# Attention outputs summed by accumulating transfers; weight casts, differences and value products moved

## The chip, the cores and the metric

The kernel runs on one core of a Trainium2 chip. A core has five engines that run side by side, each through its own queue in order: TensorE (matrix products, transposes), VectorE (elementwise work, scans), ScalarE (activations and copies), GpSimd or POOL (small elementwise work, and transfers that its software describes) and SyncE or SP (which only issues transfers). Transfers can be issued from SP's, ScalarE's and POOL's queue; the instruction that issues one waits in its queue until its data are there. Instructions wait for one another by semaphores. The metric is device time in microseconds (us) of one execution.

## The reference

The reference is one layer of a model with 1024 tokens of width 1024, in float32. Two branches run on the same normalised input, a gate merges them, and a feed-forward block follows:

```
u = rmsnorm(x) @ w_in          # q,k,v (8 heads of 64); f,i,q,g (4 heads of 128); 2 gates of 1024
o_sb = stick_breaking_attention(q_sb, k_sb, v_sb)
o_hg = rmsnorm(hgrn2(silu(q_hg), f_raw, i_hg)) * silu(g_hg)
merged = sigmoid(gate_sb + b) * (o_sb @ w_o_sb) + sigmoid(gate_hg + b) * (o_hg @ w_o_hg)
h = x + merged @ w_out
out = rmsnorm(h + square(relu(rmsnorm(h) @ w_ff1)) @ w_ff2)
```

The attention has no softmax. With z = q.k / 8, the weight of key s for query t is sigmoid(z_ts) times the product of (1 - sigmoid(z_tj)) over the keys j between s and t, for s < t only. The output of a head is the weights times v.

## The kernel before

Precision. Each float32 operand of a large product is kept as two halves: hi, a cast on ScalarE (hi_copy, line 156), and lo, the difference between the value and its hi on VectorE (lo_sub, line 161). A product is then three matmuls (hi.hi, hi.lo, lo.hi; the helper three). All matmuls are recorded at line 128 and all transposes at line 131, so the profile tells them apart by tile names.

Order. The program is traced by Python; each instruction gets a place on its engine from a planner that goes by program order and estimated times. after(a, b) forces a behind b on the same engine, without a wait. Two lanes order TensorE: the main lane (scores, transposes, value products of the attention) and the fill lane, a Stream of jobs that project the normalised input by slices of w_in. st.advance(n, upto) runs n steps of the Stream; a projection job has nine steps, eight of them with six matmuls of 512 columns. When a job starts, the Stream loads and splits the weights of the next one (prefetch). Raw weights lie in two buffers, tag "raw", their halves in two buffers each, tags "whi" and "wlo". All loads are issued from SP's queue, in the order in which they are traced (load, line 136).

Stages. First the input is normalised, transposed (norm_transpose, tiles xnt, xnh, xnl) and projected to v (pjv, units wv), with head 0's q and k. Then the attention runs over 64 items (head, block of 128 queries), the blocks in the order 7, 0, 6, 1, 5, 2, 4, 3. For an item, scores makes z, and ScalarE its two sigmoids bt and rm (lines 786 and 789); weights runs the running product as a scan on VectorE (line 808) and multiplies (line 169); turn transposes the weights (tiles pw) and splits them into wTh and wTl; values, called when both query blocks of a 256-query column qc are turned, multiplies them with v (tile po). The jobs in this stage are q and k of the heads 1 to 7 (units wqk), the f and q projections of the recurrence (wf, wq), and two of ten "raw" gate units (wga8 and wga9). The HGRN2 recurrence with the job of i (unit wi, four pieces) follows, then gates, the output projection, and the feed-forward.

The value products. v is stored as hi and lo side by side in the 128 columns of the stationary operand, so po is 128 x 256: partitions 0 to 63 hold the part with v's hi and 64 to 127 that with its lo. Their sum is the output. values copies the one half on ScalarE to the partitions of the other (line 886, tile ot), adds on VectorE (line 887, tile osb, one slot for two heads), and after the eighth column block of a pair of heads a transfer on POOL's queue stores osb to the buffer od (line 896), which is loaded again in the gate stage.

The raw gate units. A RawUnit has two raw pieces, ra and rb. split makes hi and lo of ra. split_t makes a difference rb = ra - rb (1024 wide, recorded at line 1243), a second one of its halves (512 wide, line 1243), and hi and lo of that (tile t). In the Stream it is owed from the start of the job before and paid when that job reaches step 6, all at once, the first difference behind the latest turn's lo (or, in the recurrence, behind its latest product).

The pieces of wi. hg_levels(0), the first head of the recurrence, calls u_i.split(1), which loads and splits the first piece; its cast has no place behind anything on ScalarE.

Of the kernel before, what the change touches and what calls it, by code (L numbers as in the profile page):

```python
# [10 lines left out]
F32R = mybir.dt.float32r  # L11
# [3 lines left out]
ALU = mybir.AluOpType  # L15
# [4 lines left out]
P = 128  # L20
T = 1024
D = 1024
NT = T // P
# [4 lines left out]
DHS = 64  # L28
# [11 lines left out]
def kernel(  # L40
# [19 lines left out]
    nc = tc.nc  # L60
# [14 lines left out]
    def slot(name, dt=F32):  # L75
        return spool.tile([P, 1024], dt, tag="s", name=name)

    def slot_n(name, n, dt=F32):

        if n <= 512:  # L80
            return hpool.tile([P, 512], dt, tag="h", name=name)
        return slot(name, dt)

    def bank(name):
        return psum.tile([P, 512], F32, tag="p", name=name)
# [7 lines left out]
    def dram(name, shape):  # L93
        return scratch.tile(shape, F32, tag=name, name=name)

    class Lane:
        def __init__(self):
            self.ends = []
            self.last = None
            self.gates = ()  # L100
# [4 lines left out]
    def after(ins, earlier):  # L105
        if earlier is not None and earlier.ins is not ins.ins:
            tc.add_manual_dep(ins.ins, earlier.ins.name, NOSYNC, reason="issue order")
        return ins

    def open_block(name):  # L110
        cur[0] = name
        lane = lanes[name]
        lane.gates = (lane.last,)
        if name == "main":
            lane.ends.append(lane.last)
        else:
            ends = lanes["main"].ends
            lane.gates += tuple(ends[-AHEAD : len(ends) - AHEAD + 1])
# [8 lines left out]
    def matmul(*a, **k):  # L127
        return pe(nc.tensor.matmul(*a, **k))  # L128
# [24 lines left out]
    hi_behind, hi_last, turn_hi = [None], [None], [None]  # L153

    def hi_copy(dst, src):
        hi_last[0] = after(in_turn("act", nc.scalar.copy(dst, src)), hi_behind[0])  # L156

    def lo_sub(dst, src, hi):
        return in_turn(
            "dve",  # L160
            nc.vector.tensor_tensor(out=dst, in0=src, in1=hi.bitcast(F32), op=ALU.subtract),  # L161
        )

    def hi_lo(h, l, src):
        hi_copy(h, src)
        return lo_sub(l, src, h)

    def mul(out, a, b):
        return nc.vector.tensor_tensor(out=out, in0=a, in1=b, op=ALU.mult)  # L169
# [140 lines left out]
    def norm_transpose(acts, half, b0, n, between=None):  # L310

        banks = {}

        def turn_block(kt, b):
            if kt not in banks:
                banks[kt] = bank(f"xnt{half}{kt}_{b0}")[:, 0 : n * P]
            open_block("main")
            transpose(
                banks[kt][:, b * P : (b + 1) * P],
                xt[4 * half + b0 + b][:, kt * P : (kt + 1) * P],  # L320
            )

        ahead = 6 if between else 0
        for kt in range(ahead):
            turn_block(kt, 0)
        if between:
            between()
        for kt in range(KT):
            hi, lo = acts.t.get((half, kt // 2)) or acts.make(half, kt // 2)
            cs = slice(kt % 2 * 512 + b0 * P, kt % 2 * 512 + (b0 + n) * P)  # L330
            for b in range(n):
                if b > 0 or kt >= ahead:
                    turn_block(kt, b)
            pb = banks[kt]
            g = prm[:, G1 + kt : G1 + kt + 1]
            in_turn("act", nc.scalar.activation(hi[:, cs], pb, AF.Identity, scale=g))
            in_turn(
                "dve",
                nc.vector.scalar_tensor_tensor(
                    out=lo[:, cs],  # L340
                    in0=pb,
                    scalar=g,
                    in1=hi[:, cs].bitcast(F32),
                    op0=ALU.mult,
                    op1=ALU.subtract,
                ),
            )
# [85 lines left out]
    class Unit:  # L433
# [5 lines left out]
        def split_t(self):  # L439
            pass  # L440
# [46 lines left out]
    class Stream:  # L487
# [36 lines left out]
        def step(self):  # L524

            if self.gen is None:
                if self.pos >= len(self.jobs):
                    return False
                self.steps = 0
                self._start()  # L530
            self.steps += 1
            if self.owed_t and self.steps == 6:
                self.owed_t.split_t(hg_level[0] or turn_lo[0])
                self.owed_t = None
            open_block("fill")
            if next(self.gen, StopIteration) is StopIteration:
                self.gen = None
                self.pos += 1
            return True
# [11 lines left out]
    st = Stream()  # L551
# [88 lines left out]
    def norm1(tbs):  # L640
        for tb in tbs:
            t = xt[tb]
            r = token_rstd(t, f"n1_{tb}", slot(f"n1scr{tb}"))
            in_turn(
                "dve",
                nc.vector.tensor_scalar(out=t, in0=t, scalar1=r, scalar2=None, op0=ALU.mult),
            )


    vt, qk, osb = {}, {}, {}  # L650
# [9 lines left out]
    def v_stat(h, tb):  # L660
        c = ((tb % 2) * 4 + h % 4) * P
        return vt[h // 4, tb // 2][:, c : c + P]
# [102 lines left out]
    lastsel, turn_lo = [None], [None]  # L765
# [99 lines left out]
    to_come, od = {}, {}  # L865

    def values(h, qc):
        open_block("main")
        tiles = wTt.pop((h, qc))
        nkb = 2 * qc + 2  # L870
        po = bank(f"po{h}_{qc}")[:, 0:256]
        for kb in range(nkb):
            for i in range(2):
                matmul(
                    po,
                    v_stat(h, kb),
                    tiles[kb // 4][i][:, kb % 4, :],
                    start=kb == 0 and i == 0,
                    stop=kb == nkb - 1 and i == 1,
                )  # L880
        pair, r = h // 2, (h % 2) * DHS
        if pair not in osb:
            osb[pair] = slot(f"osb{pair}")
        other = DHS - r
        tmp = slot_n(f"ot{h}_{qc}", 256)[:, 0:256]
        nc.scalar.copy(tmp[r : r + DHS, :], po[other : other + DHS, :])
        nc.vector.tensor_tensor(
            out=osb[pair][r : r + DHS, qc * 256 : (qc + 1) * 256],
            in0=po[r : r + DHS, :],
            in1=tmp[r : r + DHS, :],  # L890
            op=ALU.add,
        )
        to_come[h] = to_come.get(h, NT // 2) - 1
        if r and to_come[h] == 0:
            od[pair] = dram(f"od{pair}", [P, 1024])
            nc.gpsimd.dma_start(od[pair], osb.pop(pair))


    hg, ohg = {}, {}
    hg_sum, hg_level = [None], [None]  # L900
# [115 lines left out]
    def hg_levels(h):  # L1016
# [59 lines left out]
        for _, cs in halves():  # L1076
            after(mul(q[:, cs], q[:, cs], dec[:, cs]), pairs[3])
        if h == 0:
            u_i.split(1)
        yield  # L1080
        for l in range(7):
            H = 1 << l
# [159 lines left out]
    def sub(out, a, b):  # L1242
        return nc.vector.tensor_tensor(out=out, in0=a, in1=b, op=ALU.subtract)
# [40 lines left out]
    class RawUnit(Unit):  # L1284


        late = True

        def __init__(self, cb):
            dmas = [  # L1290
# [15 lines left out]
            hi_lo(h, l, ra)  # L1306
            self.hl = [(h, l)]

        def split_t(self, behind=None):
            if len(self.hl) == 1:  # L1310
                ra, rb = self.raw
                after(sub(rb, ra, rb), behind)
                sub(rb[:, 512:], rb[:, 512:], rb[:, 0:512])
                t = slot(f"{self.name}t", F32R)
                self.hl.append((t[:, 0:512], t[:, 512:]))
                hi_lo(*self.hl[1], self.raw[1][:, 512:])

    raw_units = [RawUnit(cb) for cb in range(NG)]

# [957 lines left out]
    st.advance(4, 1)  # L2277
    u_v.split(2)
    norm1((2, 3))
    st.advance(3, 1)  # L2280
    norm_transpose(xn, 0, 2, 2)
    u_v.split()
    st.advance(5, 1)
    norm1(range(4, NT))
    st.advance(8, 1)
    norm_transpose(xn, 1, 0, 4)
# [16 lines left out]
    for i, it in enumerate(items):  # L2303
# [16 lines left out]
        r = turn(*it, between)  # L2320
# [7 lines left out]
    st.advance(1, j_q[2])  # L2328
    while ready:
        values(*ready.popleft())  # L2330


    FILL = (3.4, 2.0, 2.6, 2.6, 2.9)
    owed = 0.0
    for h in range(NHG + 1):
        lev = hg_levels(h) if h < NHG else iter(())
        tail = hg_tail(h - 1) if h > 0 else iter(())
        upto = (j_i, j_raw[1], j_raw[6], j_sb[1], j_sb[2])[h]
        going, turned = True, False
        while going:  # L2340
            going = False
            for g in (lev, tail):
                if g is tail and h == 1 and turned and going and st.pos < j_i:
                    continue
                turned = turned or g is tail
                if next(g, StopIteration) is not StopIteration:
                    going = True
                    owed += FILL[h]
                    st.advance(int(owed), upto)
                    owed -= int(owed)  # L2350
        if h + 1 < NHG:
            st.finish(max(j_f[h + 1], j_q[h + 1]))
# [102 lines left out]
```

## Time and profile before

| what | value |
|---|---|
| median of 3 runs | 1439.45 us (1439.32 to 1440.04) |
| profiled execution, its own time | 1439.79 us |
| span of that execution, first to last instruction | 1437.8 us |
| granted TensorE clock | 0.999 |
| TensorE busy | 1424.4 us, 99% |
| VectorE busy | 1118.8 us, 78% |
| ScalarE busy | 678.3 us, 47% |
| POOL busy | 148.0 us, 10% |

PE is TensorE, PEld its loading of weights, DVE VectorE, ACT ScalarE; a q behind a name is the engine's queue, which issues transfers. In a row of the stretches the columns are the window and its length, busy time and count for PE, PEld, DVE, ACT and POOL, the granted clock, the share of the DMA engines and GB/s. In a row of waits: who waited for whom, the total in us, how often, the longest. In a row of the timeline: start, duration, engine, line, operation, result and operands, shapes, count, and in brackets the idle time before it and what ended it. In a row of transfers: size of one, and the median us from issue to landing.

### The profile page before, as it was taken

To read this page: it belongs to the slowest core of one execution; us is meant where nothing else is said; L and a number is where in the kernel's file an instruction comes from. 1 tells how busy PE (TensorE), PEld (TensorE's weight loads), DVE (VectorE), ACT (ScalarE), POOL (GpSimd) and SP (SyncE) were. 2 spreads that over 40 slices of the span, in tenths; PEclk is the share of its full clock that TensorE was granted. 3 is DMA by queue.
4 is the path that set the end of the run, shared out by engine and by line. 5 is a ranking of instruction groups with operands and counts; after the bars stand their busy time and mean duration, and the time that the engine had idled before them with its cause. 6 is when DMAs were issued, how large, how long until landed. Compare 5 with 4: busy or idle time off the path is not lost.

```text
span 1437.8 us, 19221 instructions
## 1 busy us (share of the span) xinstructions
PE 1424.4 (99%) x7056; PEld 1194.5 (83%) x7056; DVE 1118.8 (78%) x1537; ACT 678.3 (47%) x1177; POOL 148.0 (10%) x338
## 2 busy tenths in 40 slices
PE   9999999999999999999999999999999999999998
PEld 8888888888888888888888888888888888888886
DVE  6579999989678898798787898666666758668765
ACT  6356676663233345333244674444444433524343
POOL 3011223210011031000000300000000000000042
PEclk9999999999999999999999999999999999999999
DMA  7124435534015775545477405344446974776835
GB/s 238 27 62 115 110 85 92 89 60 133 22 45 154 232 184 196 167 158 180 153 275 249 176 31 197 131 143 145 161 153 212 349 264 164 259 275 253 274 103 182
DMA packets 161334, 233.54 MB, mean 162 GB/s; under 512 B 26028, under 2 KB 93144, under 8 KB 161240
## 3 DMA queue, kind: packets, MB, share of 16 engines
q1 hardware_dynamic: 145400, 190.11, 39.4%
q0 software_dynamic: 11520, 34.61, 9.4%
q10 hardware_dynamic: 4320, 7.60, 1.4%
q8 instruction: 55, 0.90, 0.3%
q14 instruction: 39, 0.32, 0.1%
HBM read 167.27 MB, written 65.01 MB: 162 GB/s over the span
## 4 chain that ended last, share of the span: by engine, by line
PE 92%; DVE 4%; ACT 1%; DMA 1%; issue 1%; POOL 0%; SPq 0%; DVEq 0%; ACTq 0%; POOLq 0%
PE pm L128 21%; PE pX L128 9%; PE pW L128 6%; PE pY L128 6%; PE pjqk L128 5%; PE gX L128 4%; PE gY L128 4%; PE pga L128 3%; PE pys L128 3%; PE pji L128 3%; PE pyh L128 3%; PE pjq L128 3%; PE pjv L128 3%; PE sl L128 3%; PE pwX L128 2%; PE po L128 2%
## 5 line engine op out<-in xcount | busy, mean ns | idle before, releaser
L156 ACT CAST whid<-w 128x1024 fp32r<-128x1024 f32 x30 | 31.6, 1054 | 154.6 <-PE pm L128 90.0
L808 DVE TENSOR_TENSOR_SCAN rm<-rm,bits 128x511 f32<-128x511 f32 (+7 forms) x72 | 87.1, 1218 | 9.6 <-ACT rm L786 9.4
L128 PE MATMUL pm<-wlod,sh 128*128 128x512 f32 x240 | 93.5, 390 | 0.0
L128 PE MATMUL pm<-whid,sl 128*128 128x512 f32 x240 | 93.4, 389 | 0.0
L128 PE MATMUL pm<-whid,sh 128*128 128x512 f32 x240 | 93.4, 389 | 0.0
L128 PE MATMUL pm<-tl,sh 128*128 128x512 f32 (+1 forms) x210 | 81.3, 387 | 0.0
L128 PE MATMUL pm<-th,sl 128*128 128x512 f32 (+1 forms) x210 | 81.3, 387 | 0.0
L128 PE MATMUL pm<-th,sh 128*128 128x512 f32 (+1 forms) x210 | 81.3, 387 | 0.0
L161 DVE TENSOR_TENSOR wlod<-w,whid 128x1024 fp32r<-128x1024 f32 x30 | 36.7, 1222 | 55.0 <-ACT whid L156 55.0
L161 DVE TENSOR_TENSOR sl<-sa,sh 128x1024 fp32r<-128x1024 f32 x56 | 68.2, 1218 | 0.0
L156 ACT CAST wTh<-pw 128x512 fp32r<-128x512 f32 (+2 forms) x96 | 43.9, 487 | 40.8 <-PE pw L131 39.6
L2091 POOL TENSOR_SCALAR fss<-fss 128x1 f32<-128x1 f32 x8 | 4.5, 560 | 562.1 <-ACT fsc L2086 561.6
L156 ACT CAST sh<-sa 128x1024 fp32r<-128x1024 f32 x56 | 57.2, 1046 | 6.1 <-DMA sa<-ad 6.1
L161 DVE TENSOR_TENSOR wTl<-pw,wTh 128x512 fp32r<-128x512 f32 (+2 forms) x96 | 50.5, 547 | 4.9 <-ACT wTh L156 4.6
L128 PEld LDWEIGHTS pm<-wlod,sh 128*128 128x128 f32 x240 | 45.1, 188 | 10.0 <-DVE wlod L161 0.4
L128 PEld LDWEIGHTS pm<-whid,sh 128*128 128x128 f32 x240 | 45.0, 187 | 9.4
L128 PEld LDWEIGHTS pm<-whid,sl 128*128 128x128 f32 x240 | 45.1, 188 | 9.1
L169 DVE TENSOR_TENSOR bt<-bt,rm 128x511 f32<-128x511 f32 (+7 forms) x72 | 49.0, 684 | 4.2 <-DVE rm L808 0.5
L128 PE MATMUL pX<-sql,t1h 128*128 128x512 f32 x128 | 50.0, 391 | 0.1
L128 PE MATMUL pX<-sqh,t1h 128*128 128x512 f32 x128 | 49.8, 389 | 0.0
L128 PE MATMUL pX<-sqh,t1l 128*128 128x512 f32 x128 | 49.8, 389 | 0.0
L786 ACT ACTIVATE rm<-z 128x511 f32<-128x511 f32 (+4 forms) x96 | 48.0, 500 | 3.5 <-DVE wTl L161 1.0
(933 smaller groups left out, 4475.5 us busy)
## 6 DMA issues: line engine op xcount, KB each, us to landing
w<-in_w_ff_dram SPq DMA_DIRECT2D x72, 512.0 KB, 6.2
sa<-ad SPq DMA_DIRECT2D x56, 512.0 KB, 7.0
ad<-a SPq DMA_DIRECT2D x32, 256.0 KB, 2.1
ad<-s SPq DMA_DIRECT2D x16, 512.0 KB, 5.5
tw<-in_w_out_dram POOLq DMA_DIRECT2D x24, 256.0 KB, 4.0
pr<-pd SPq DMA_DIRECT2D x10, 512.0 KB, 5.1
x<-in_x_dram SPq DMA_DIRECT2D x8, 512.0 KB, 9.9
xnl<-xnh POOLq DMA_DIRECT2D x8, 512.0 KB, 8.9
```

What stands on the lines that cost most here:

```text
L128: return pe(nc.tensor.matmul(*a, **k))
L156: hi_last[0] = after(in_turn("act", nc.scalar.copy(dst, src)), hi_behind[0])
L161: nc.vector.tensor_tensor(out=dst, in0=src, in1=hi.bitcast(F32), op=ALU.subtract),
L169: return nc.vector.tensor_tensor(out=out, in0=a, in1=b, op=ALU.mult)
L786: nc.scalar.activation(rm[:, s0 + c0 - 1 : s0 + m - 1], z[:, c0:m], AF.Sigmoid, scale=-0.125)
L808: sc = nc.vector.tensor_tensor_scan(out=rr, data0=rr, data1=bits[:, 1024 - nk + a : 1024 - nk + b][:, ::-1], initial=rm[:, b : b + 1] if i ...
L2091: nc.gpsimd.tensor_scalar(out=ssq, in0=ssq, scalar1=1.0 / D, scalar2=EPS, op0=ALU.mult, op1=ALU.add)
```

## The change

Four things are changed; no matmul is added or taken out.

- The two halves of the attention output. values now copies the whole of po (128 x 256) on ScalarE into a slot osb of its own for each head. When a head's four column blocks are there, a transfer on POOL's queue adds partitions 64 to 127 onto partitions 0 to 63 within SBUF. The store to od follows per head: keep_attended issues it from ScalarE's queue, right behind the next head's first copy, and for the last head from SP's queue. The adds on VectorE and the tiles ot are gone.
- split_t is paid in three pieces, at steps 4, 6 and 8 of the job before: the first difference, the second, and the cast with its lo; each is put behind the latest turn's lo (or the recurrence's product).
- The cast of u_i's first piece is put behind the last turn's hi cast.
- At the start, the Stream takes four steps instead of three before the second transposes, and four instead of five after them: four matmuls of v's lo move ahead of these transposes.

```diff
--- before.py
+++ after.py
@@ -529,9 +529,10 @@
                 self.steps = 0
                 self._start()
             self.steps += 1
-            if self.owed_t and self.steps == 6:
-                self.owed_t.split_t(hg_level[0] or turn_lo[0])
-                self.owed_t = None
+            if self.owed_t and self.steps in (4, 6, 8):
+                self.owed_t.split_t(hg_level[0] or turn_lo[0], self.steps // 2 - 1)
+                if self.steps == 8:
+                    self.owed_t = None
             open_block("fill")
             if next(self.gen, StopIteration) is StopIteration:
                 self.gen = None
@@ -878,22 +879,25 @@
                     start=kb == 0 and i == 0,
                     stop=kb == nkb - 1 and i == 1,
                 )
-        pair, r = h // 2, (h % 2) * DHS
-        if pair not in osb:
-            osb[pair] = slot(f"osb{pair}")
-        other = DHS - r
-        tmp = slot_n(f"ot{h}_{qc}", 256)[:, 0:256]
-        nc.scalar.copy(tmp[r : r + DHS, :], po[other : other + DHS, :])
-        nc.vector.tensor_tensor(
-            out=osb[pair][r : r + DHS, qc * 256 : (qc + 1) * 256],
-            in0=po[r : r + DHS, :],
-            in1=tmp[r : r + DHS, :],
-            op=ALU.add,
-        )
-        to_come[h] = to_come.get(h, NT // 2) - 1
-        if r and to_come[h] == 0:
-            od[pair] = dram(f"od{pair}", [P, 1024])
-            nc.gpsimd.dma_start(od[pair], osb.pop(pair))
+        if to_come.get(h) is None:
+            to_come[h] = NT // 2
+            osb[h] = slot(f"osb{h}")
+        nc.scalar.copy(osb[h][:, qc * 256 : (qc + 1) * 256], po)
+        to_come[h] -= 1
+        keep_attended()
+        if to_come[h] == 0:
+            nc.gpsimd.dma_start(osb[h][0:DHS, :], osb[h][DHS:P, :], accum_op=ALU.add)
+            summed.append(h)
+
+    summed = []
+
+    def keep_attended(queue=nc.scalar):
+        while summed:
+            h = summed.pop()
+            pair, r = h // 2, (h % 2) * DHS
+            if r == 0:
+                od[pair] = dram(f"od{pair}", [P, 1024])
+            queue.dma_start(od[pair][r : r + DHS, :], osb.pop(h)[0:DHS, :])
 
 
     hg, ohg = {}, {}
@@ -1076,7 +1080,9 @@
         for _, cs in halves():
             after(mul(q[:, cs], q[:, cs], dec[:, cs]), pairs[3])
         if h == 0:
+            hi_behind[0] = turn_hi[0]
             u_i.split(1)
+            hi_behind[0] = None
         yield
         for l in range(7):
             H = 1 << l
@@ -1285,6 +1291,7 @@
 
 
         late = True
+        turned = 0
 
         def __init__(self, cb):
             dmas = [
@@ -1306,14 +1313,18 @@
             hi_lo(h, l, ra)
             self.hl = [(h, l)]
 
-        def split_t(self, behind=None):
-            if len(self.hl) == 1:
-                ra, rb = self.raw
-                after(sub(rb, ra, rb), behind)
-                sub(rb[:, 512:], rb[:, 512:], rb[:, 0:512])
-                t = slot(f"{self.name}t", F32R)
-                self.hl.append((t[:, 0:512], t[:, 512:]))
-                hi_lo(*self.hl[1], self.raw[1][:, 512:])
+        def split_t(self, behind=None, upto=3):
+            ra, rb = self.raw
+            while self.turned < upto:
+                self.turned += 1
+                if self.turned == 1:
+                    after(sub(rb, ra, rb), behind)
+                elif self.turned == 2:
+                    after(sub(rb[:, 512:], rb[:, 512:], rb[:, 0:512]), behind)
+                else:
+                    t = slot(f"{self.name}t", F32R)
+                    self.hl.append((t[:, 0:512], t[:, 512:]))
+                    after(hi_lo(*self.hl[1], rb[:, 512:]), behind)
 
     raw_units = [RawUnit(cb) for cb in range(NG)]
 
@@ -2277,10 +2288,10 @@
     st.advance(4, 1)
     u_v.split(2)
     norm1((2, 3))
-    st.advance(3, 1)
+    st.advance(4, 1)
     norm_transpose(xn, 0, 2, 2)
     u_v.split()
-    st.advance(5, 1)
+    st.advance(4, 1)
     norm1(range(4, NT))
     st.advance(8, 1)
     norm_transpose(xn, 1, 0, 4)
@@ -2328,6 +2339,7 @@
     st.advance(1, j_q[2])
     while ready:
         values(*ready.popleft())
+    keep_attended(nc.sync)
 
 
     FILL = (3.4, 2.0, 2.6, 2.6, 2.9)
```

## The prediction

> **What bounds the kernel now.** I read the page first, then the busy times by stretch, then who waited for whom on TensorE, and last the order of time around each wait that these named.
>
> ```profile
> span 1437.8 us, 19221 instructions
> ...
> PE 1424.4 (99%) x7056; PEld 1194.5 (83%) x7056; DVE 1118.8 (78%) x1537; ACT 678.3 (47%) x1177; POOL 148.0 (10%) x338
> ...
> PE 92%; DVE 4%; ACT 1%; DMA 1%; issue 1%; POOL 0%; SPq 0%; DVEq 0%; ACTq 0%; POOLq 0%
> ```
> ```profile
> 80.00:340.00 260.00, 256.59 (x1454) 220.45 (x1453) 239.41 (x345) 174.53 (x385) 55.84 (x191) 1.00 0.42 96
> ...
> 640.00:660.00 20.00, 20.00 (x90) 16.57 (x89) 17.23 (x27) 8.46 (x11) 1.08 (x2) 1.00 0.51 174
> ```
> ```profile
> PE po L128 <- DVE wTl L161: 2.0, 6, 0.5
> PE po L128 <- ACT wTh L156: 1.4, 2, 0.9
> PE pjqk L128 <- DVE xnl L339: 0.3, 1, 0.3
> PE xnt L131 <- DVE xnl L339: 0.2, 1, 0.2
> PE xnt L131 <- DVE x L646: 0.2, 1, 0.2
> ```
>
> TensorE is the bound: busy 99% of the span and 92% of the chain that ended last. The change takes no matmul out and adds none, so it can win only time in which TensorE stands. That time is small and it sits in the part that the change touches. In the attention stretch (80 to 340 us) TensorE is busy 256.59 of 260.00, so 3.41 us idle, which is just what the first two wait rows sum to (2.0 + 1.4). In the late stretch quoted beside it there is none; there 90 matmuls of 512 columns start in 20.00 us, a pitch of 0.222 us, and the granted clock is 1.00 in both. So a matmul of 256 columns has a pitch of about 0.11 us (half; an estimate). VectorE is busy 239.41 of 260.00 (92%) in that stretch and ScalarE 174.53 (67%): VectorE is the engine that has no room there.
>
> All waits of TensorE in the stretch are of one kind: a value product (po) that wants the hi cast (wTh, ScalarE) or the lo difference (wTl, VectorE) of the weights just transposed. Two places hold most of it. The first:
>
> ```profile
> 102.88 1.21 DVE L1243 TENSOR_TENSOR wga8r<-wga8r,wga8r 128x1024 f32<-128x1024 f32 x1
> ...
> 105.14 0.66 DVE L1243 TENSOR_TENSOR wga8r<-wga8r 128x512 f32<-128x512 f32 x1
> ...
> 106.49 0.69 DVE L161 TENSOR_TENSOR wga8t<-wga8r,wga8t 128x512 fp32r<-128x512 f32 x1
> ...
> 105.83 0.62 ACT L156 CAST wga8t<-wga8r 128x512 fp32r<-128x512 f32 x1 [3.02 <-DVE wga8r L1243]
> ...
> 105.92 0.60 PE L131 MATMUL pw<-ident,bt 128*128 128x128 f32 x4
> 106.99 0.38 PE L128 MATMUL po<-wTh,V 128*128 128x256 f32 x1 [0.48 <-ACT wTh L156]
> 107.83 0.39 PE L128 MATMUL po<-wTl,V 128*128 128x256 f32 x1 [0.46 <-DVE wTl L161]
> ```
>
> Here split_t of gate unit 8 stands in the way. ScalarE waits 3.02 us for the second difference of wga8r, with the casts of the attention weights queued behind that wait; then VectorE runs wga8t's lo before the wTl that TensorE wants. The second:
>
> ```profile
> 320.43 1.05 ACT L156 CAST wih<-wir 128x1024 fp32r<-128x1024 f32 x1 [4.84 <-DMA wir<-in_w_in_dram]
> ...
> 321.89 0.56 DVE L161 TENSOR_TENSOR wTl<-pw,wTh 128x384 fp32r<-128x384 f32 x1 [2.96 <-ACT wTh L156]
> ...
> 321.88 0.60 PE L131 MATMUL pw<-ident,bt 128*128 128x128 f32 x4
> 323.37 0.38 PE L128 MATMUL po<-wTh,V 128*128 128x256 f32 x1 [0.89 <-ACT wTh L156]
> 324.10 0.39 PE L128 MATMUL po<-wTl,V 128*128 128x256 f32 x1 [0.34 <-DVE wTl L161]
> ```
>
> Here ScalarE waits 4.84 us for a load of u_i's first piece, which nobody needs yet, while three casts of the last turns stand behind it; VectorE then waits 2.96 us, and TensorE pays.
>
> The rows of the start, which the moved value products touch:
>
> ```profile
> 16.76 1.07 PE L128 MATMUL pjv<-wvl,xnh 128*128 128x512 f32 x4
> 17.67 0.27 PE L131 MATMUL xnt<-ident,x 128*128 128x128 f32 x1
> 18.14 1.20 PE L131 MATMUL xnt<-ident,x 128*128 128x128 f32 x9 [0.20 <-DVE x L646]
> 19.55 0.83 PE L131 MATMUL xnt<-ident,x 128*128 128x128 f32 x4 [0.21 <-DVE xnl L339]
> ```
>
> Nine transposes take 1.20 us with the last one's 0.27 in it, so their pitch is (1.20 - 0.27) / 8 = 0.116 us.
>
> **The change part by part.**
>
> split_t in three pieces (steps 4, 6 and 8 of the job before, each behind the latest turn's lo). No instruction is added; the 1024-wide difference goes some steps earlier, the cast and its lo some steps later. At the first place the differences are then over when ScalarE comes to the cast, and wga8t's lo is no longer just ahead of wTl. From the first transpose at 105.92 to the second po at 107.83 are 1.91 us; undisturbed it would be 4 x 0.116 + 0.11 = 0.57. That is 1.34 us lost; the idle figures alone give 0.48 + 0.46 = 0.94. I take 1.34, since start to start is what moves everything behind it. What is late next: the raw buffers of units 8 and 9 come free only when the last lo has read them, and SP issues loads in order:
>
> ```profile
> 107.21 1.02 SPq L136 DMA_DIRECT2D wqk4r<-in_w_in_dram  x2
> ...
> 314.67 17.25 SPq L136 DMA_DIRECT2D wir<-in_w_in_dram  x4
> ```
>
> Both start just as a wga lo ends (106.49 + 0.69 = 107.18 for the first). Two steps later in the job is some 3 us later here, for wqk4 and for the first piece of wi. wqk4 is a unit ahead, and wi is wanted by no matmul before the attention is over, so I cost this at nothing; if that cover is gone, it is one wait like those above, about 1.3 us.
>
> u_i's first cast behind the last turn's hi. Nothing added, one order. ScalarE no longer stands at 315.6 to 320.4, the casts of the last turns go when their transposes end, and the po at 323.37 finds its operands. From 321.88 to 324.10 are 2.22 us against 0.57, so 1.65 lost; by idle figures 0.89 + 0.34 = 1.23. I take 1.65. Later the same cast costs its 1.05 us on ScalarE behind the turns, where no po is queued behind it.
>
> The attention outputs.
>
> ```profile
> L886 ACT COPY ot<-po x32: 364/368/371, 93.9 to 332.5; 64x256 f32<-64x256 f32 x32
> L887 DVE TENSOR_TENSOR osb<-po,ot x32: 406/422/429, 94.8 to 332.9; 64x256 f32<-64x256 f32 x32
> ```
>
> ScalarE keeps 32 copies, now 128 partitions instead of 64 at the same 256 columns, which I cost the same, 0.368 us each. VectorE loses 32 adds of 0.422 = 13.5 us out of its 239.41: 92% busy becomes 87%. The po bank also comes free after the copy and not after the add, and a half slot for ot goes while a full slot for osb stays a little longer at each change of head. What it is worth on TensorE: besides the two places above, po waits for wTl four more times, 2.0 - 0.46 - 0.34 = 1.2 us in all. That bounds the gain at 1.2; the bound from the other side is nothing, or a loss where another order puts a 1.2 us lo of a weight ahead of a wTl. These four stand behind casts and differences of the next weights more than behind adds, so I take a quarter, 0.3.
>
> What it adds: 8 accumulating transfers on POOL's queue instead of 4 stores, and 8 stores, 7 on ScalarE's queue and the last on SP's.
>
> ```profile
> xnl<-xnh POOLq DMA_DIRECT2D x8, 512.0 KB, 8.9
> ...
> tw<-tw POOLq DMA_DIRECT2D x8, 256.0 KB, 5.5
> ...
> od<-osb POOLq DMA_DIRECT2D x4, 512.0 KB, 3.5
> ```
> ```profile
> L1379 POOL DMA_DIRECT2D xnl<-xnh x8: 853/878/2217, 431.0 to 529.2; - x8
> ...
> DMA to landing us min/median/max: 4.6/8.9/13.5
> ```
> ```profile
> 324.00 0.33 ACTq L1346 DMA_DIRECT2D pd<-p  x1
> ...
> 299.61 0.37 ACT L886 COPY ot<-po 64x256 f32<-64x256 f32 x1
> ...
> 309.40 0.37 ACT L886 COPY ot<-po 64x256 f32<-64x256 f32 x1 [1.53 <-PE po L128]
> ```
>
> POOL: 8 x 0.878 instead of 4 stores, some 5 us more on an engine that is busy 55.84 of 260.00, and it waits for a ScalarE copy instead of a VectorE add: nothing. ScalarE's sequencer: 7 x 0.33 = 2.3 us of issuing; with 67% busy I take nothing, and 2.3 as the far end, if each stood right ahead of a wTh that TensorE wants. The new wait is the one to watch: the store sits on ScalarE's queue behind the first copy of the next head, and casts and sigmoids of the next items queue behind it. The tightest of the changes of head is quoted: from the copy's end at 299.98 to the next head's copy's end at 309.77 are 9.8 us, less about 0.9 for POOL's issue and what POOL needs to notice, some 8.5 us for the transfer to land. 256 KB accumulated from HBM took 5.5 us in the median and 512 KB within SBUF 8.9, with 4.6 as the least and 13.5 as the most; I take 5.5, the row of the same size, and nothing is waited for.
>
> The Trainium skill, "SBUF — State Buffer", section "Door 1: The DMA port swizzle", states that 64 partitions in a row reach only half of the memory's DMA ports, so that they get the bandwidth of 32. By that rule these 256 KB would take what 512 KB over 128 partitions take, 8.9 and not 5.5 us, and ScalarE would stand 0.4 us in the tightest gap; at the price below that is 0.1 us, and the sum would be 3.4 and not 3.5. No run here shows it yet.
>
> The start. One step, four matmuls of 512 columns (4 x 0.222 = 0.9 us), goes from among the second transposes to ahead of them. It covers the 0.20 us for x; it takes cover from the transposes that wait for banks (0.21), which the next job steps can give back. Far ends: 0.4 gained, 0.9 lost if all eight casts slip. I take 0.2 gained.
>
> Sum: 1.34 + 1.65 + 0.3 + 0.2 = 3.5 us. The profiled run took 1439.79 us, 1.99 more than its span of 1437.8, and 0.34 more than the median 1439.45. So 1439.45 - 3.5, about 1436.0.
>
> **The rivals.**
>
> The waits move on (no clear change). VectorE stays near 90%, the order of all engines shifts, and pieces of split_t now stand in front of some other po. For it: four such waits exist already without any split_t, 0.3 us idle each, 1.2 / 4. If two or three fresh ones the size of the first place come up (1.34, or 0.94 by idle), the gain is 3.5 - 2 = 1.5 or less: 1438.0. Against it: the two big ones have causes that the change takes away by name.
>
> All of it goes. If VectorE's 13.5 us clear the four others as well and the start wins its 0.4: 1.34 + 1.65 + 1.2 + 0.4 = 4.6, with a little from matmuls not marked as waiting 5.5: 1434.0.
>
> Slower: the store on ScalarE's queue waits for the accumulating transfer. Place: the first copy of heads 1 to 7. Price: the 4.84 us wait at 320 cost 1.65 us of TensorE, so 0.34 per us waited. If transfers land 13.5 us after issue, the wait is 5 us, 7 x 5 x 0.34 = 12 us, and the time 1439.45 - 3.5 + 12 = 1448; at 11.2 us (2.7 waited) it is 6.4 us, and 2.9 us slower than before: from there on the change is a loss. For it: the slowest row. Against it: that row is of pairs of 512 KB issued back to back; the others have more than 8.5 us.
>
> **How the numbers follow.** A measurement of this kernel can tell about 0.2% from no change, 2.9 us, so faster is under 1436.6 and slower over 1442.3. The forecast has 0.48, all of it gone 0.07 (both faster, 0.55); waits that move on 0.27 (within); the late store and mishaps of order like it 0.18 (slower). The likeliest case by itself runs from 1434.8 to 1437 (idle figures instead of start to start: 3.5 - 0.8 = 2.7). The range for 8 in 10 reaches down to 1433.2, past the case where all goes, and up to 1441.5, over the moved waits and a mild late store; the strong late store is left out.
>
> **What would show it.** Right: no ScalarE wait for wga8r near 103 to 106 and none for wir before the last wTh; TensorE idle in the attention stretch near 1 us, with VectorE about 13 us less busy; no wait of ScalarE on the accumulating transfer. Wrong: TensorE idle again near 3.4 us with other names (moved waits); a row of ScalarE waiting for osb by DMA of several us (late store); TensorE idle above 1 us between 17 and 25 us (the start).

## The result, and the profile after

The changed kernel takes 1435.78 us in the median (1435.38 to 1436.77, 9 runs) against 1439.63 (1439.32 to 1440.38, 9 runs) on the same chip: 3.85 us less, ratio 0.9974, 95% interval 0.9965 to 0.9982. Forecast were 1436.0 us, in 1433.2 to 1441.5. The profiled execution took 1435.38 us with a span of 1433.5, 4.3 less than before's.

The page of the changed kernel, and under it the attention stretch and who waited for whom on TensorE:

```profile
span 1433.5 us, 19215 instructions
...
PE 1422.9 (99%) x7056; PEld 1194.9 (83%) x7056; DVE 1105.2 (77%) x1505; ACT 675.9 (47%) x1177; POOL 150.5 (10%) x342
...
PE 97%; DVE 1%; DMA 1%; ACT 1%; issue 0%; POOL 0%; SPq 0%; ACTq 0%; DVEq 0%
```
```profile
80.00:340.00 260.00, 259.10 (x1472) 223.82 (x1471) 230.59 (x319) 173.54 (x387) 59.09 (x195) 1.00 0.48 106
```
```profile
PE po L128 <- DVE wTl L161: 0.9, 2, 0.6
PE xnt L131 <- DVE xnl L339: 0.2, 1, 0.2
PE pjqk L128 <- DVE xnl L339: 0.2, 1, 0.2
```

TensorE is idle 0.90 us in the attention stretch, after 3.41; VectorE is busy 230.59 us there, after 239.41 (over the whole run 1105.2 after 1118.8, so 13.6 less). The po waits went from eight to two. TensorE's share of the chain rose from 92% to 97%.

The first place (timeline of the changed kernel, rows of VectorE, ScalarE and TensorE):

```profile
98.43 1.22 DVE L1249 TENSOR_TENSOR wga8r<-wga8r,wga8r 128x1024 f32<-128x1024 f32 x1
...
103.21 0.68 DVE L1249 TENSOR_TENSOR wga8r<-wga8r 128x512 f32<-128x512 f32 x1
...
107.71 0.67 DVE L161 TENSOR_TENSOR wga8t<-wga8r,wga8t 128x512 fp32r<-128x512 f32 x1
```
```profile
103.92 0.62 ACT L156 CAST wga8t<-wga8r 128x512 fp32r<-128x512 f32 x1 [1.28 <-DVE wga8r L1249]
```
```profile
105.73 0.60 PE L131 MATMUL pw<-ident,bt 128*128 128x128 f32 x4
106.09 0.36 PE L128 MATMUL po<-wTh,V 128*128 128x256 f32 x1
106.45 0.38 PE L128 MATMUL po<-wTl,V 128*128 128x256 f32 x1
```

The differences come at 98.4 and 103.2 instead of 102.9 and 105.1, ScalarE waits 1.28 us instead of 3.02, and wga8t's lo runs after the value products have begun. From the first transpose to the second po are 0.72 us instead of 1.91.

The second place:

```profile
319.60 0.60 PE L131 MATMUL pw<-ident,bt 128*128 128x128 f32 x4
319.95 0.36 PE L128 MATMUL po<-wTh,V 128*128 128x256 f32 x1
320.15 0.28 PE L128 MATMUL po<-wTl,V 128*128 128x256 f32 x1
```
```profile
320.72 1.05 ACT L156 CAST wih<-wir 128x1024 fp32r<-128x1024 f32 x1
```

The cast of wi's first piece comes after the last turn's casts, and from the first transpose to the second po are 0.55 us instead of 2.22.

The start:

```profile
16.80 1.98 PE L128 MATMUL pjv<-wvl,xnh 128*128 128x512 f32 x8
18.61 1.25 PE L131 MATMUL xnt<-ident,x 128*128 128x128 f32 x10
20.08 0.83 PE L131 MATMUL xnt<-ident,x 128*128 128x128 f32 x4 [0.21 <-DVE xnl L339]
```

The wait for x is gone, the one for xnl stays, as the prediction had it. Between 17 and 25 us TensorE is busy 7.79 us, after 7.59: 0.2 us, the term of the sum.

What is new (first the osb tile's instructions and the accumulating transfer's landing, min/median/max; then the timeline around the one large wait that is left):

```profile
L885 ACT COPY osb<-po x32: 371/373/393, 93.7 to 328.2; 128x256 f32<-128x256 f32 x32
L889 POOL DMA_DIRECT2D osb<-osb x8: 830/844/879, 113.7 to 328.9; - x8
L900 ACTq DMA_DIRECT2D od<-osb x7: 452/453/498, 117.3 to 301.4; - x7
```
```profile
DMA to landing us min/median/max: 3.5/3.5/5.2
```
```profile
209.03 0.45 ACTq L900 DMA_DIRECT2D od<-osb  x1
209.53 0.60 ACT L787 ACTIVATE rm<-z 128x511 f32<-128x511 f32 x1 [2.69 <-DMA osb<-osb]
...
210.92 1.75 DVE L809 TENSOR_TENSOR_SCAN rm<-rm,bits 128x767 f32<-128x767 f32 x1 [2.70 <-ACT rm L787]
...
214.04 1.14 DVE L161 TENSOR_TENSOR wTl<-pw,wTh 128x512 fp32r<-128x512 f32 x2
...
214.77 0.38 PE L128 MATMUL po<-wTl,V 128*128 128x256 f32 x1 [0.58 <-DVE wTl L161]
```

The full copies cost 0.373 us each against 0.368 for half the partitions. The transfer lands 3.5 us after its issue. The store does not sit behind the next head's first copy, as the section on the change has it: the planner set it some 4 us after the head's last copy (117.28 after 113.04 for head 0), probably where its estimate has the transfer landed. Once, near 207 us, the transfer took 5.2 us and ScalarE stood 2.69 us; VectorE then stood 2.70 for its scan's input, and TensorE 0.58 (from one po's start at 213.82 to the next at 214.77 are 0.95 us, 0.83 over its pitch). The list of waits names this one alone, but there are more: the stores at 147.06, 177.73 and 270.13 us are also issued just as their transfers land (3.5 us after the issues at 143.52, 174.18 and 266.59), and ScalarE stands 1.29, 1.00 and 0.97 us around them, against 0.2 to 0.3 in the run below that issues the stores later. The profile puts these down to other engines; by the table below no matmul is late behind them.

### The profile page after: what moved, and what is told of

Same layout as the page of the kernel before. It is cut to its first block, busy times and chain, and to the rows that moved or that the text cites. A ratio compares the mean times of both kernels' runs of the same rounds, so it can differ in the third digit from the quotient of the medians.

```text
span 1433.5 us, 19215 instructions
## 1 busy us (share of the span) xinstructions
PE 1422.9 (99%) x7056; PEld 1194.9 (83%) x7056; DVE 1105.2 (77%) x1505; ACT 675.9 (47%) x1177; POOL 150.5 (10%) x342
## 4 chain that ended last, share of the span: by engine, by line
PE 97%; DVE 1%; DMA 1%; ACT 1%; issue 0%; POOL 0%; SPq 0%; ACTq 0%; DVEq 0%
PE pm L128 21%; PE pX L128 9%; PE pW L128 6%; PE pY L128 6%; PE pjqk L128 5%; PE pga L128 4%; PE gX L128 4%; PE gY L128 4%; PE pjf L128 3%; PE pys L128 3%; PE pji L128 3%; PE pjq L128 3%; PE pjv L128 3%; PE pyh L128 3%; PE po L128 3%; PE sl L128 3%
```

## The experiments

All times are medians; "less" is against the kernel before, run beside it. The diffs are excerpts, and some calls in them are shortened. For the po waits I also give the time lost from start to start: the distance between the starts of two neighbouring matmuls less the median distance for that shape in the same kernel, where it is over 0.24 us. This is what each place cost:

| kernel | 91 | 106 | 122 | 168 | 184 | 214 | 261 | 322 | sum |
|---|---|---|---|---|---|---|---|---|---|
| before | 0.48 | 1.36 | 0.47 | - | 0.53 | - | 0.51 | 1.66 | 5.0 |
| changed | 0.48 | 0.25 | - | - | - | 0.83 | - | - | 1.6 |
| outputs alone | 0.48 | 0.96 | - | - | - | 0.79 | - | - | 2.2 |
| all but outputs | 0.47 | 0.68 | 0.57 | - | 0.53 | - | 0.50 | - | 2.8 |
| split_t alone | 0.48 | 0.68 | 0.56 | - | 0.53 | - | 0.48 | 1.04 | 3.8 |
| u_i's cast alone | 0.48 | 1.36 | 0.45 | - | 0.52 | - | 0.51 | - | 3.3 |
| changed, adds kept | 0.48 | 0.57 | 0.72 | 0.55 | 0.52 | - | - | - | 2.8 |
| changed, u_i's cast as before | 0.48 | 0.24 | - | - | - | 1.08 | - | - | 1.8 |
| changed, stores held back | 0.48 | 0.25 | - | - | 0.58 | - | - | - | 1.3 |

(columns: us from the span's start, rounded; the places shift by up to 4 us between kernels. One profiled run each; the same place differs by some tenths between two runs of one program: 0.83 and 0.98 near 214 us for the changed kernel.)

**All but the attention outputs.**

```diff
-        nc.scalar.copy(osb[h][:, qc * 256 : (qc + 1) * 256], po)
+        nc.scalar.copy(tmp[r : r + DHS, :], po[other : other + DHS, :])
+        nc.vector.tensor_tensor(out=osb[pair][...], in0=po[r : r + DHS, :], in1=tmp[r : r + DHS, :], op=ALU.add)
```

> The changed kernel with the attention outputs added on VectorE again, as before; split_t in three pieces, u_i's cast behind the last turn and the start stay changed. Theory of the prediction (the two ScalarE waits are the gain): 1.34 + 1.65 + 0.2 = 3.2 us under the kernel before, so about 1436.4 us, and TensorE idle in the attention stretch near 1 us. Rival (the gain is VectorE's 13.5 us of adds, without which its queue is too full for the waits to go): half of it or less, 1438 us or more, and several waits of po for wTl back in the attention stretch.

Measured: 1436.94 against 1439.36, 2.4 less, ratio 0.9983 (0.9974 to 0.9992); TensorE idle 1.76 us in the attention stretch. Between the two: both ScalarE waits are gone from TensorE's list, but the po waits for wTl at 106, 122, 184 and 261 us are there.

```profile
PE po L128 <- DVE wTl L161: 1.8, 5, 0.4
```
```profile
98.46 0.41 DVE L888 TENSOR_TENSOR osb<-po,ot 64x256 f32<-64x256 f32 x1
98.79 1.21 DVE L1246 TENSOR_TENSOR wga8r<-wga8r,wga8r 128x1024 f32<-128x1024 f32 x1
...
106.08 0.88 DVE L161 TENSOR_TENSOR wTl<-pw,wTh 128x512 fp32r<-128x512 f32 x2
```
```profile
106.82 0.38 PE L128 MATMUL po<-wTl,V 128*128 128x256 f32 x1 [0.44 <-DVE wTl L161]
```

From 96.8 to 106.9 us VectorE never stands by the profile, an add of 0.41 us among its work, and it comes to wTl just too late. The changed kernel has the same instructions in the same order there, from 96.76 us on, without the add, and the same row reads

```profile
105.72 0.88 DVE L161 TENSOR_TENSOR wTl<-pw,wTh 128x512 fp32r<-128x512 f32 x2
```

One add at 98.46 us thus makes a lo 0.36 us later that starts 7.6 us behind it, and the place costs 0.68 instead of 0.25. So split_t in pieces frees ScalarE, while the larger part of what is left there belongs to VectorE's queue.

**The attention outputs alone.** The kernel before with the changed values, keep_attended and the call at the end.

> The kernel before with only the attention outputs changed (ScalarE copies all of po, transfer adds the halves, store per head). Theory of the prediction: 0.3 us of gain, and up to 0.8 us lost where a store on ScalarE's queue stands before its transfer has landed, so 1439.3 to 1440.2 us; ScalarE's waits for wga8r and wir are still there. Rival (VectorE's 13.5 us are the gain): 2 us or more under the kernel before, 1437.6 us or less.

Measured: 1436.38 against 1439.36, 2.98 less, ratio 0.9979 (0.9970 to 0.9988). The rival's time came: this part alone gives 2.98 of 3.85, though neither u_i's cast nor split_t was touched. Of ScalarE's two waits, which should both stay, the one for wga8r is there (2.6 us) and the one for wir is not.

```profile
80.00:340.00 260.00, 258.60 (x1468) 223.19 (x1468) 231.29 (x320) 174.17 (x387) 59.21 (x195) 1.00 0.48 106
```
```profile
PE po L128 <- DVE wTl L161: 1.3, 3, 0.5
```
```profile
313.69 13.87 SPq L136 DMA_DIRECT2D wir<-in_w_in_dram  x4
```
```profile
317.49 1.05 ACT L156 CAST wih<-wir 128x1024 fp32r<-128x1024 f32 x1 [0.23 <-DMA wir<-in_w_in_dram]
```

It also removed the wait near 322 us, by a way the prediction did not see: VectorE ends wga9t's lo at 313.66 instead of 314.64, SP starts the load of wi at 313.69 instead of 314.67, it lands by 317.5 instead of 320.4, and ScalarE stands 0.23 us instead of 4.84. The earlier start is the small part of this. TensorE is ahead by more, as waits are gone before: it begins the transposes of this place at 320.62 instead of 321.88, so the load starts 6.93 us ahead of them instead of 7.21. Two other things changed. The load itself takes 3.7 us instead of 5.7 (the view of the transfers with their time from issue to landing, first from 314.6 to 320.5 us before, then from 313.6 to 317.6 us here):

```profile
q0 software_dynamic: 149, 0.26, 24.7%
...
wir<-in_w_in_dram SPq DMA_DIRECT2D x1, 512.0 KB, 5.7
```
```profile
wir<-in_w_in_dram SPq DMA_DIRECT2D x1, 512.0 KB, 3.7
```

Before, 0.26 MB of POOL's queue (q0) moved beside it, behind two transfers tw issued at 310.08 and 311.19 us; here the last tw was issued at 308.63, and q0 moved nothing. And the order on ScalarE is another: one of the three casts that stood behind wih's is ahead of it now, 316.28 against 317.49 (first before, then here).

```profile
321.38 0.47 ACT L156 CAST wTh<-pw 128x384 fp32r<-128x384 f32 x1
```
```profile
316.28 0.47 ACT L156 CAST wTh<-pw 128x384 fp32r<-128x384 f32 x1
```

Which of the two clears the place, and whether the transfers beside it slowed the load, was not tested. The one place had two remedies.

**split_t in three pieces alone.**

```diff
-            if self.owed_t and self.steps == 6:
+            if self.owed_t and self.steps in (4, 6, 8):
```

> The kernel before with split_t in three pieces alone. Theory of the prediction: 1.3 us less, about 1438.3 us; no long ScalarE wait for wga8r, the po near 107 us waits under 0.3 us, the waits near 322 us stay. Rival (waits only move on while VectorE is 92% busy): within 0.4 us of the kernel before, with a new po wait for wTl of about 1 us elsewhere.

Measured: 1438.66 against 1439.36, 0.70 less, ratio 0.9995 (0.9986 to 1.0004), not to be told from none by the interval. The trace has half of the 1.34: the wait for wTh at 106 us is gone, that for wTl stays (0.68 of 1.36), over the 0.3 that was expected. The place near 322 us, which should stay as it was, fell from 1.66 to 1.04: the cast of the 128x384 weights is ahead of wih's here too. No new wait came up, so the rival did not come either.

**u_i's cast behind the last turn alone.**

```diff
+            hi_behind[0] = turn_hi[0]
             u_i.split(1)
+            hi_behind[0] = None
```

> The kernel before with u_i's first cast behind the last turn's hi alone. Theory of the prediction: 1.65 us less, about 1438.0 us; TensorE does not wait near 322 us, the waits near 107 us stay. Rival (VectorE is then late with wTl in its place): 0.5 us less or nothing, and po near 322 us waits for wTl.

Measured: 1437.79 against 1439.36, 1.57 less, ratio 0.9989 (0.9981 to 0.9998). By itself the term is near the forecast, 1.65, and the place near 322 us is clean. That place is not the same in every run: with only the start changed, which does not touch it, it cost 1.38 instead of 1.66 (wi's load took 5.4 us there).

**The start alone.**

```diff
-    st.advance(3, 1)
+    st.advance(4, 1)
     norm_transpose(xn, 0, 2, 2)
     u_v.split()
-    st.advance(5, 1)
+    st.advance(4, 1)
```

> The kernel before with only the start changed (four steps before the second transposes instead of three). Theory of the prediction: 0.2 us less, far ends 0.4 less and 0.9 more; the wait for x near 18 us is gone and the wait for xnl near 20 us stays. Rival: the moved step only takes cover from the transposes, nothing or up to 0.9 us more.

Measured: 1439.35 against 1439.72, ratio 0.9997 (0.9988 to 1.0006): 0.4 us less, not resolved. In the trace the wait for x is gone, the one for xnl stays, and TensorE is busy 7.79 us between 17 and 25 us, after 7.59.

**The changed kernel without the order of u_i's cast.**

> The changed kernel with u_i's first cast again without a place behind the last turn. By the prediction's separate terms: 1.65 us over the changed kernel, about 1437.2 us, and po waits near 320 us. By the overlap seen in the kernel with the accumulating transfers alone (VectorE frees the raw buffer sooner, the load of wi starts and lands sooner, and ScalarE's wait for it ends before po wants its operands): at most 0.4 us over it, 1435.4 to 1435.9 us, and no po wait near 320 us.

Measured: 1435.70 against 1439.52, ratio 0.9973 (0.9964 to 0.9983), inside the range of the overlap: 3.82 less, where the whole change had 3.85 less in its first measurement and 4.18 in a second. ScalarE waits 0.98 us for wi, and po near 320 us does not:

```profile
317.41 1.05 ACT L156 CAST wih<-wir 128x1024 fp32r<-128x1024 f32 x1 [0.98 <-DMA wir<-in_w_in_dram]
```
```profile
320.15 0.36 PE L128 MATMUL po<-wTh,V 128*128 128x256 f32 x1
320.35 0.28 PE L128 MATMUL po<-wTl,V 128*128 128x256 f32 x1
```

So the order that is worth 1.57 us by itself is worth nothing that can be measured once the adds are gone and split_t is in pieces.

**The changed kernel with the adds kept as extra work.**

```diff
+        extra = slot_n(f"ot{h}_{qc}", 256)[:, 0:256]
+        nc.vector.tensor_tensor(out=extra[0:DHS, :], in0=po[0:DHS, :], in1=osb[h][0:DHS, cs], op=ALU.add)
```

> The changed kernel with 32 adds of 64x256 still on VectorE as extra work (their results are not used); ScalarE's copies, the transfers and the stores as changed. If VectorE's load is what brought back the po waits near 122, 184 and 261 us and the rest of the one near 106 us, the changed kernel loses what it had over the kernel without the accumulating transfers, 1 us or more: 1436.8 to 1438 us, with these waits back. If it is only another order of the instructions, or the po bank that comes free earlier, the time stays at 1435.8 us.

Measured: 1437.46 against 1439.72, 2.3 less, ratio 0.9983 (0.9974 to 0.9992), so about 1.6 us of the gain are given back, about as much as by leaving out the transfers (1.4). All 11 runs are slower (1436.98 and more) than the slowest of the changed kernel (1436.77). The place at 106 us costs more again (0.57 after 0.25), the waits at 122 and 184 us return, one at 168 comes up, the one at 261 does not return, and the one at 214 is gone.

```profile
80.00:340.00 260.00, 258.25 (x1464) 222.07 (x1463) 237.63 (x347) 172.47 (x385) 60.43 (x195) 1.00 0.48 104
```
```profile
PE po L128 <- DVE wTl L161: 1.7, 5, 0.5
```

So these 1.6 us hang on the adds being gone; ScalarE's copies and POOL's transfers are still there and do not bring it by themselves. It isn't a clean test of VectorE's load: the extra adds also hold the po bank and the transfer (which waits for them), and the planner's order changes with them. The later transfers make ScalarE stand for them three times by the list, 6.5 us in all instead of 2.7, once just ahead of the place at 122 us:

```profile
121.00 0.97 ACT L156 CAST wTh<-pw 128x512 fp32r<-128x512 f32 x2 [2.81 <-DMA osb<-osb]
```

That wTh is what the late wTl at 122 us needs, so the wait there can be the transfer's as well as VectorE's. Near 184 us it is the order (below). The one place that shows the load by itself is 106 us, by the pair of rows under "All but the attention outputs".

**The stores behind the next head's first copy.**

```diff
-            queue.dma_start(od[pair][r : r + DHS, :], osb.pop(h)[0:DHS, :])
+            after(queue.dma_start(od[pair][r : r + DHS, :], osb.pop(h)[0:DHS, :]), behind)
```

> The changed kernel with each store on ScalarE's queue held behind the next head's first copy (which the prediction took to be so already; the trace shows the planner sets stores 4 to 6 us after the head's last copy). Theory: the 2.69 us that ScalarE waits for the transfer near 207 us is what makes po wait near 214 us, so ScalarE waits for no transfer of osb and 0.8 us go: about 1435.0 us. Rival: the po wait near 214 us comes from VectorE's own queue there and stays: 1435.8 us.

Measured: 1435.40 against 1439.72, ratio 0.9968 (0.9957 to 0.9980). No wait of ScalarE for a transfer is left and the po wait near 214 us is gone, so that wait was the store's. But one near 182 us came up:

```profile
180.57 1.20 DVE L161 TENSOR_TENSOR wqk6l<-wqk6r,wqk6h 128x1024 fp32r<-128x1024 f32 x1
181.69 0.69 DVE L169 TENSOR_TENSOR q<-qx,q 128x512 f32<-128x512 f32 x1
182.29 1.15 DVE L161 TENSOR_TENSOR wTl<-pw,wTh 128x512 fp32r<-128x512 f32 x2
```
```profile
183.03 0.38 PE L128 MATMUL po<-wTl,V 128*128 128x256 f32 x1 [0.41 <-DVE wTl L161]
```

In the changed kernel wqk6's lo stands behind that wTl, here again ahead of it, as in the kernel before. So of the three small waits that the outputs cleared (122, 184 and 261 us), the one at 184 us was cleared by order: it is here without any add on VectorE.

To compare, the three places for the stores ran on one chip:

> The changed kernel itself, beside its two variants on one chip: 3.8 us under the kernel before, as measured first; the wait of ScalarE for an osb transfer near 207 us and the po wait near 214 us are there again.

> The stores held behind the next head's first copy, once more beside the changed kernel. Theory: the wait near 214 us is gone (0.83 us start to start), but a wait near 182 us came up in its place (0.58 us), so 0.2 to 0.4 us under the changed kernel. Rival: the two cost the same, within 0.2 us.

> The changed kernel with the seven stores issued from POOL's queue instead of ScalarE's. Theory (a wait on POOL's queue costs less, as POOL is busy 59 of 260 us): no ScalarE wait for a transfer, no po wait near 214 us, 0.3 to 0.8 us under the changed kernel. Rival: the memsets of bt and wT and the copies of QH and QL queue behind each store on POOL, and TensorE waits for them: 1 us or more over the changed kernel.

```diff
-    def keep_attended(queue=nc.scalar):
+    def keep_attended(queue=nc.gpsimd):
```

Against 1439.52: the changed kernel 1435.34 (ratio 0.9970, 0.9959 to 0.9982), the stores behind the copy 1435.40 (0.9971, 0.9960 to 0.9982), the stores on POOL's queue 1435.56 (0.9971, 0.9960 to 0.9982). The three are the same, so the rival of the second expectation came. The changed kernel's two waits are there again (ScalarE 2.8 us, po 0.98). The stores held back lose 0.3 to 0.6 us less in the attention stretch by the trace, and the time is no shorter: a wait that goes there is not always won in the whole. On POOL's queue the waits are there and harm nobody on ScalarE:

```profile
POOL od L900 <- DMA osb<-osb: 8.4, 4, 3.5
```

Neither expectation came, not 0.3 to 0.8 us under and not 1 us or more over: the po wait near 214 us goes and the one near 182 us comes, as with the stores held back. No version beats the changed kernel by what can be measured.

**The store at once, with the casts behind it.**

```diff
             summed.append(h)
+            if h < NHS - 1:
+                hi_behind[0] = keep_attended()
```

> The changed kernel with each of the seven stores on ScalarE's queue set right behind its transfer's issue, and all later casts held behind the store, so that ScalarE stands until the transfer has landed (about 4.5 us at each of seven changes of head). It measures the price of the slower rival. By the prediction's price of 0.34 us per us that ScalarE waits: 7 x 4.5 x 0.34 = 10.7 us more, about 1446.5 us. If ScalarE's idle time takes most of it, as it is 67% busy there, 3 us more or less: at most 1439 us.

Measured: 1442.11 against 1439.72, 2.4 more, ratio 1.0018 (1.0010 to 1.0027), and 2.39 + 3.85 = 6.2 more than the changed kernel: between the two expectations.

```profile
ACT wTh L156 <- DMA osb<-osb: 18.2, 5, 5.1
```
```profile
PE po L128 <- DVE wTl L161: 4.3, 6, 1.2
```

The list names five waits, 18.2 us. The other two stand under other names, right behind their stores at 117.64 and 148.37 us (2.19 and 3.66); the second is

```profile
148.86 0.59 ACT L156 CAST wTh<-pw 128x512 fp32r<-128x512 f32 x1 [3.66 <-DVE bt L169]
```

So ScalarE stood at all seven, 24.0 us in all, 3.4 each instead of 4.5, and 6.2 / 24.0 = 0.26 us of TensorE per us that ScalarE stands. In the changed kernel it stands some 5 us around its stores already (2.69, and some 2.5 at the three others over what it stands there without a store); against the 19 us that come on top it is 0.33. The price in the prediction, 0.34, is at the upper end of this.

## Why the prediction was right, and where its steps were not

The total is right, 3.5 us forecast and 3.85 measured, but its largest parts are in another place than it said.

- "These four stand behind casts and differences of the next weights more than behind adds, so I take a quarter, 0.3": the step that failed. The outputs alone are worth 2.98 us, not 0.3. By the table they take away 2.8 us: three of the four small waits go whole (122, 184 and 261 us, 1.5 together), the first place gives 0.40 and the second 1.66, and 0.79 comes up near 214. So not a quarter of the four went but three, and the bound of 1.2 left out that the outputs also act at the two places that were counted elsewhere. I read each wait back only to the instruction just ahead of it on VectorE. At 106 us the runs show what that misses: an add 7.6 us earlier makes wTl 0.36 us later, as VectorE does not stand in between. For the other places this is not shown: near 184 us it was the order, near 261 the adds come back without the wait, and near 322 the shorter load and the order of the casts, with the earlier start a small part.
- split_t: ScalarE's part of the mechanism is as described, the term was half: 1.34 forecast, 0.70 measured alone (not resolved, and by the trace not all of it from this place), 0.68 left at the place. I took both of its waits for one cause; the second was in good part VectorE's queue. Only with the adds gone does the place fall to 0.25.
- u_i's cast: 1.65 forecast, 1.57 alone. But it does not add up with the rest: in the whole change it is worth nothing that shows. The four parts alone give 2.98 + 0.70 + 1.57 + 0.37 = 5.6 us (the second and the last not resolved), the whole 3.85. Two remedies for one wait count once; the prediction's sum was near the truth because the term too low and the terms that overlap cancel. That is luck.
- The start: 0.2 forecast; the wait that should go went, and the time moved by 0.4 at most, within what can be told from nothing.
- The late store: it is real, and near the price (0.83 for 2.69 us, 0.31), but it came through a mistake of mine. I had the store behind the next head's copy, with 8.5 us of cover; the planner put it some 4 us behind the last copy, when the transfer is just landing. It cost 0.83 us at one of seven changes of head; at three more ScalarE stood some 0.7 to 1 us and TensorE lost nothing. Holding it back removes that wait and brings another.
- The landing: I took 5.5 us, the row of the same size; it was 3.5. By the Trainium skill, "SBUF — State Buffer", "Door 1: The DMA port swizzle", I had made that 8.9, by taking the row of the 512 KB transfers for 256 KB; the measurement decides against that use of the rule. Those were not all in pairs, as I had read: of the eight, two were issued at 431.03 and 432.39 us, one at 518.79, the others between 521.94 and 529.2 us, 1.0 to 3.3 us apart. That this made them slow is likely, not shown. Whether 64 partitions cost bandwidth here no run shows.
- SP's loads behind the later wga lo: no new wait for wqk4 or wi appeared on TensorE, as costed (wi's load even starts earlier, at 313.47 after 314.67).
- The signs: TensorE's idle time near 1 us (0.90) and VectorE's 13 us less came. Two did not: ScalarE still waits 1.28 us for wga8r, and 2.69 us for a transfer of osb.

## What to carry to other kernels

Where an engine is as busy as VectorE here (92%), follow a wait back to the last time that engine stood, and count every instruction since then, also those that look unrelated: the change that took 0.42 us from each of 32 places was worth more here than either repair made right at the waits, in part by the new order that it brought. Price repairs of the same wait as alternatives and not as a sum, and undo them one by one from the finished version to see which still counts. When an instruction is only "issued later" in the program, look in the order that the planner makes where it really stands before counting its cover. And when an engine stands just behind the issue of a store, compare the time with the landing that the store waits for: the list of waits may name another engine.

## What the runs showed that I had not expected

A wait on a load of one unit (wi, ScalarE 4.84 us) was ended by a change that touches neither the load nor the cast: the load started 0.98 us sooner and landed 2.9 us sooner (wih's cast could start at 317.5 instead of 320.4). The 2 us between them are the load's own time. Where the profile gives it, it is 5.7 and 5.4 us in the two kernels where 0.26 MB of POOL's queue moved beside it (before, and with only the start changed), and 3.7 us in three where 0.03 MB or nothing did (the outputs alone, split_t alone, the changed kernel with u_i's cast as before). That the one makes the other is likely, not tested. And a copy out of the accumulators on ScalarE costs the same for 128 partitions as for 64 (0.373 against 0.368 us at 256 columns), so moving both halves in one copy was free.
